# Where the large SBUF tiles of a gated decoder layer begin, counted in bytes

## Chip, core and metric

The kernel runs on one core of a Trainium2 chip. The metric is the device time of one execution in microseconds (us). Before the change three runs took 1215.79, 1216.19 and 1220.27 us; the median is 1216.19 us.

## The reference, cut to what matters

One decoder layer over 1024 positions, model width 1024, everything in float32:

```python
h = rmsnorm(x, mix_norm)
q, k, v, su, sv, g_a, g_b = split(h @ w_in)
y_att = sliding_window_attention(q, k, v, q_norm, k_norm, sinks)   # window 128, ALiBi, sinks
y_sgu = chunked_spatial_gating(su, sv, sgu_norm, w_s, b_s)         # chunks of 128
merged = sigmoid(g_a) * (y_att @ w_oa) + sigmoid(g_b) * (y_sgu @ w_ob)
x = x + merged @ w_out
z = causal_conv3(rmsnorm(x, ffn_norm) @ w_up)                      # 1024 x 5632
gate, val = split(z)
x = x + (silu(gate) * val) @ w_down
```

## The kernel before

**Precision.** TensorE is fed with `float32r`. To keep float32 accuracy each operand is split into a high part and a low part, and each product is three matmuls: high by high, high by low, low by high (`mm3`, lines 79 to 81). Every matmul loads its own 128x128 stationary operand (the trace calls that LDWEIGHTS, on the row PEld), also when the next one uses the same again. The moving operand is 512 columns wide in the large stages and 256 in the projections for k, v, q and the gating input.

**Stages, in the order of time.** First the projections for k and v while x arrives. Then attention over 128-query blocks, with the q and u projections as filler work of TensorE. Then the gating input v (`v_half`, line 531: 256-column matmuls with moving tiles `wv` and `wvB`, stationary x). From about 261 us on all large work is in 512-column matmuls: 8 gate pairs, 16 branch products `po` (24 matmuls each), 8 output products `px` (48 each), 22 pairs of the MLP, and the down projection. The gate pairs and the MLP pairs use seven block products instead of eight (`Blocks.prod`, line 914: A11, A12, S1, A22, S2, S3, S4, of 12 matmuls each); the down projection uses seven as well (line 1595, 924 matmuls).

**Pools.** SBUF is handed out by pools, from the left and from the right, and each tile begins where the pool puts it. The tiles that TensorE reads come from these pools:

- `big` with tag `Y`: seven tiles of 16 KB in each partition, for the activations x, T1 to T4 and B, for `wq`, `wv`, `wkv`, for mh, ml, and for all four operands of the down projection (`ah`, `al`, `bh`, `bl`).
- `wst`, the weight pool: tiles `wh` and `wl` (line 93) of 4 KB, two of each; in the trace `ph`, `qh`, `wjh` are high parts and `pl`, `ql`, `wjl` low parts.
- S2 and S4 of the pairs (`AX`, `gax`) and S3 (`s3h`, `s3l`) are stationary operands too, but don't come from the weight pool: `AX` is a `Y` tile, the others are from smaller pools.
- `zr`, on the right: `wvB`, and later T3 of the gate pairs.

In the built program these tiles begin, as a remainder by 256 bytes:

```
Y tiles, wh, wl, s3h, s3l, gax, T3 of the MLP, vsh, vsl     32
wvB and T3 of the gate pairs (pool zr)                     224
ch, cl, eh, el of attention                                 64
```

All slices that a matmul takes of them are whole multiples of 512 bytes away from the tile's begin, so the remainder holds for each matmul's operand. Remainders 32 and 224 are both 32 by 64 bytes.

**Order.** The order of TensorE's work, and most of the others', is the order of the code (`manual_schedule`). Waits come from the tiles that instructions share.

Of the kernel before, what the change touches and what calls it, by code (L numbers as in the profile page):

```python
# [10 lines left out]
F = mybir.dt.float32  # L11
R = mybir.dt.float32r
U8 = mybir.dt.uint8
# [21 lines left out]
def build(tc, a):  # L35
    nc = tc.nc
    ctx = ExitStack()
    with ctx, tc.manual_schedule(engines={mybir.EngineType.PE}):
        body(ctx, tc, nc, a)


def body(ctx, tc, nc, a):
    L, H = slice(0, 512), slice(512, 1024)
    base = ctx.enter_context(tc.tile_pool(name="base", bufs=1))
    big = ctx.enter_context(tc.tile_pool(name="big", bufs=1))
    wst = ctx.enter_context(tc.tile_pool(name="wst", bufs=2))
    uid = [0]
# [26 lines left out]
    def copy_hi(dst, src, scale=1.0):  # L74
        return nc.scalar.activation(dst, src, AF.Copy, scale=scale)  # L75
# [37 lines left out]
    def rsqrt_cols(dst, ss, n, width):  # L113

        nc.vector.tensor_scalar(dst, ss, 1.0 / width, EPS, op0=ALU.mult, op1=ALU.add)
        return nc.gpsimd.tensor_tensor(dst, dst, mh05[:, :n], op=ALU.pow)

    msk = base.tile([128, 4, 128], U8, name="msk")

    def rms_rows(pb, diag, hs=(0, 1)):  # L120

# [2 lines left out]
        for h, p in zip(hs, pb):  # L124
# [9 lines left out]
    att = tc.tile_pool(name="att", bufs=1)  # L134
    at = att.__enter__()
    vhl = at.tile([128, 8, 2, 128], R, name="vhl")
    kgq = at.tile([128, 1], F, name="kgq")
    eps_x = at.tile([128, 8], F, name="eps_x")
    nsink = at.tile([128, 8], F, name="nsink")
    kp_cm = tc.tile_pool(name="kp", bufs=1, side="right")  # L140
    kp = kp_cm.__enter__()
    kTh = kp.tile([128, 2, 1024], R, name="kTh")
    kTl = kp.tile([128, 1024], R, name="kTl")
    ali = kp.tile([128, 8, 128], F, name="ali")
    nc.gpsimd.affine_select(out=ali[:, 0:4, :], in_=ones.unsqueeze(1).to_broadcast([128, 4, 128]),
                            pattern=[[0, 4], [1, 128]], compare_op=ALU.is_gt, fill=0.0, base=0,
                            channel_multiplier=-1)
# [40 lines left out]
    def xsquare(k):  # L188
        for c in (L, H):
            xs = xr[k][:, 257 + c.start:257 + c.stop]  # L190
            if k == 0:
                nc.scalar.activation(sqsum[:, c], xs, AF.Square)
                continue
            sq = PH("sq")
            nc.scalar.activation(sq, xs, AF.Square)
            nc.vector.tensor_tensor(sqsum[:, c], sqsum[:, c], sq, op=ALU.add)
# [35 lines left out]
        if k == 6:  # L232
            rsplit(wq[0], rwq[1], 1)
    xsquare(7)
    u_next = [wst.tile([128, 8, 128], R, tag="wh", name="u0h"), wst.tile([128, 8, 128], R, tag="wl", name="u0l")]
    copy_hi(u_next[0], u_raw[0])
    nc.vector.tensor_tensor(u_next[1], u_raw[0], u_next[0].bitcast(F), op=ALU.subtract)

# [1033 lines left out]
    def ssq_cols(p):  # L1272
        for s in range(8):
            nc.tensor.matmul(p[:, 2 * s:2 * s + 2], pools["sq2"][:, s * 128:(s + 1) * 128], ones[:, 0:2],
                             start=True, stop=True)
        pool = pools["fp"]
        ss = pool.tile([128, 8], F, name="ss8b")
        nc.vector.tensor_copy(ss, p[:, 0:16].rearrange("p (s two) -> p s two", two=2)[:, :, 0])
        rsqrt_cols(ss, ss, 8, D)
        nc.vector.reciprocal(rstd, rstd)  # L1280
        nc.vector.tensor_tensor(ss, ss, rstd, op=ALU.mult)
        diag = pool.tile([128, 8, 128], F, tag="ac", name="diag2", bufs=2)
        nc.vector.tensor_tensor(diag, ident.unsqueeze(1).to_broadcast([128, 8, 128]),
                                ss.unsqueeze(2).to_broadcast([128, 8, 128]), op=ALU.mult)
        return diag
# [80 lines left out]
    def first_pair():  # L1366
# [34 lines left out]
        nc.vector.tensor_tensor(q.g0, q.g0, x1, op=ALU.add)  # L1401
        pb = q2.zv
        diag = ssq_cols(pb)
        nx.sums_r()
        q.prod(q.v1, "S2", "T2", more=True)
# [379 lines left out]
```

## Time and profile before

| | |
|---|---|
| median of three runs | 1216.19 us |
| span of the profiled execution | 1218.1 us |
| PE busy | 1195.9 us, 98% of the span |
| DVE busy | 893.3 us, 73% |
| ACT busy | 542.1 us, 45% |
| POOL busy | 568.0 us, 47% |
| mean granted TensorE clock | 0.992 |

The page gives no time of the profiled execution other than its span; it is 1.9 us above the median of the runs. Matmuls overlap in the engine's pipeline, so a matmul's listed duration (389 ns for 512 columns) is not what it costs in a stream. What it costs is the distance from one start to the next, which has to be read from start times or from a count of instructions in a stretch.

### The profile page before, as it was taken

The numbers are of one execution on the slowest core, as the hardware profiler recorded it, in microseconds if no ns is written. First come the engines' busy times: TensorE is split into PE (matmuls) and PEld (weight loads), VectorE is DVE, ScalarE is ACT, GpSimd is POOL, SyncE is SP. The second block draws the span as 40 slices with busy tenths as digits, with TensorE's granted clock in tenths as the row PEclk, the third lists the DMA queues.
The fourth block names the chain that finished last, engine by engine and source line by source line (L and its number), as shares of the span: only waits on it lengthen the run. The fifth ranks groups of instructions, "written<-read, shape, count | busy, mean of one in ns | idle before, by whom it ended". The sixth has DMA issues, their size and how long they took to land.

```text
span 1218.1 us, 15838 instructions
## 1 busy us (share of the span) xinstructions
PE 1195.9 (98%) x5866; PEld 1004.7 (82%) x5866; DVE 893.3 (73%) x1033; ACT 542.1 (45%) x830; POOL 568.0 (47%) x358
## 2 busy tenths in 40 slices
PE   9999999889999999999999999999999999999998
PEld 8888889868887888888788888888888888888886
DVE  7788866874455665577798788887888888775674
ACT  8555566733434322223444444444444445424331
POOL 2466584278766522334756657566575642000000
PEclk9999999989999999999899999999999999999999
DMA  7010133125767897442223334233332347975471
GB/s 274 26 52 19 53 121 139 42 85 169 256 237 274 289 348 286 156 156 103 96 87 121 121 113 145 88 122 117 117 141 90 124 166 274 386 253 190 143 233 66
DMA packets 78989, 191.27 MB, mean 157 GB/s; under 512 B 8896, under 2 KB 9152, under 8 KB 78912
## 3 DMA queue, kind: packets, MB, share of 16 engines
q1 hardware_dynamic: 78912, 190.26, 44.3%
q8 instruction: 46, 0.75, 0.2%
q14 instruction: 31, 0.25, 0.1%
HBM read 139.63 MB, written 50.59 MB: 156 GB/s over the span
## 4 chain that ended last, share of the span: by engine, by line
PE 87%; DVE 6%; DMA 3%; ACT 2%; issue 1%; POOL 1%; SPq 0%; ACTq 0%; DVEq 0%
PE pz L914 42%; PE pd L1595 10%; PE pdy L1595 7%; PE px L81 2%; PE px L79 2%; PE po L79 2%; PE po L81 2%; PE po L80 2%; PE px L80 2%; DMA ls<-wup 2%; PE pv L498 1%; PE pu L81 1%; PE pu L79 1%; PE pu L80 1%; DVE T L750 1%; PE pq L79 1%
## 5 line engine op out<-in xcount | busy, mean ns | idle before, releaser
L914 PE MATMUL pz<-T,qh 128*128 128x512 f32 x464 | 142.8, 389 | 0.0
L879 POOL TENSOR_TENSOR pl<-lp,ph 128x1024 fp32r<-128x1024 f32 x30 | 73.6, 2455 | 85.0 <-ACT ph L75 84.9
L914 PE MATMUL pz<-B,ph 128*128 128x512 f32 x352 | 109.5, 392 | 0.0
L914 PEld LDWEIGHTS pz<-T,qh 128*128 128x128 f32 x464 | 87.2, 188 | 18.1
L914 PE MATMUL pz<-T,ql 128*128 128x512 f32 x232 | 90.3, 389 | 0.0
L96 POOL TENSOR_TENSOR wjl<-wj,wjh 128x512 fp32r<-128x512 f32 (+1 forms) x24 | 41.1, 1713 | 95.2 <-ACT wjh L75 95.2
L879 POOL TENSOR_TENSOR ql<-lq,qh 128x1024 fp32r<-128x1024 f32 x30 | 77.5, 2582 | 14.8 <-ACT qh L75 14.8
L914 PEld LDWEIGHTS pz<-B,ph 128*128 128x128 f32 x352 | 65.3, 188 | 15.5 <-ACT x L1443 1.9
L929 DVE TENSOR_TENSOR pz<-pz,rstd_b 128x1024 f32<-128x1024 f32 x60 | 73.9, 1232 | 3.0 <-ACT rstd_b L125 0.9
L879 POOL TENSOR_TENSOR s3l<-s,s3h 128x512 fp32r<-128x512 f32 x30 | 41.2, 1374 | 71.2 <-ACT s3h L75 67.0
L914 PE MATMUL pz<-T,s3h 128*128 128x512 f32 x232 | 71.7, 390 | 0.0
L914 PE MATMUL pz<-B,pl 128*128 128x512 f32 x176 | 68.6, 390 | 0.0
L1595 PE MATMUL pd<-bh,ah 128*128 128x512 f32 x176 | 68.5, 389 | 0.0
L1595 PE MATMUL pd<-bl,ah 128*128 128x512 f32 x176 | 68.5, 389 | 0.0
L1595 PE MATMUL pd<-bh,al 128*128 128x512 f32 x176 | 68.5, 389 | 0.0
L914 PE MATMUL pz<-T,AX 128*128 128x512 f32 x264 | 65.8, 400 | 0.0
L914 PE MATMUL pz<-B,AX 128*128 128x512 f32 x264 | 63.4, 389 | 0.0
L75 ACT ACTIVATE qh<-lq 128x1024 fp32r<-128x1024 f32 x30 | 31.9, 1063 | 66.7 <-issue 46.6
L914 PEld LDWEIGHTS pz<-T,AX 128*128 128x128 f32 x264 | 51.2, 194 | 10.8
L914 PEld LDWEIGHTS pz<-B,AX 128*128 128x128 f32 x264 | 49.6, 188 | 10.3
L1301 DVE SCALAR_TENSOR_TENSOR tg<-pz,cp,tg 128x1023 f32<-128x1023 f32 (+1 forms) x44 | 56.2, 1278 | 0.8
L1301 DVE SCALAR_TENSOR_TENSOR tv<-pz,cp,tv 128x1023 f32<-128x1023 f32 (+1 forms) x44 | 56.2, 1278 | 0.8
(333 smaller groups left out, 3556.9 us busy)
## 6 DMA issues: line engine op xcount, KB each, us to landing
ls<-wup SPq DMA_DIRECT2D x22, 512.0 KB, 5.9
sum<-ls SPq DMA_DIRECT2D x22, 512.0 KB, 5.3
lp<-wup SPq DMA_DIRECT2D x22, 512.0 KB, 3.6
ra<-wdown SPq DMA_DIRECT2D x44, 256.0 KB, 4.7
b<-T SPq DMA_DIRECT2D x44, 256.0 KB, 3.7
B<-tv SPq DMA_DIRECT2D x33, 256.0 KB, 2.0
T<-tt SPq DMA_DIRECT2D x33, 256.0 KB, 2.1
b<-B SPq DMA_DIRECT2D x33, 256.0 KB, 3.4
```

The costliest lines, as they stand in the source:

```text
L75: return nc.scalar.activation(dst, src, AF.Copy, scale=scale)
L79: nc.tensor.matmul(out, wh, mh, start=first, stop=False, **kw)
L80: nc.tensor.matmul(out, wh, ml, start=False, stop=False, **kw)
L81: nc.tensor.matmul(out, wl, mh, start=False, stop=last, **kw)
L96: nc.gpsimd.tensor_tensor(l[:, :nk, :], r[:, :nk, :], h[:, :nk, :].bitcast(F), op=ALU.subtract)
L498: nc.tensor.matmul(o, vhl[:, kb, g, :], w, start=i == 0, stop=i == len(ops) - 1)
L750: nc.vector.tensor_tensor(xb[n][:, 1, kk, :], src, xb[n][:, 0, kk, :].bitcast(F), op=ALU.subtract)
L879: nc.gpsimd.tensor_tensor(l, r, h.bitcast(F), op=ALU.subtract)
L914: nc.tensor.matmul(o, p[:, k, :], y[:, q, k, :], start=not more and k == 0 and j == 0, stop=k == 3 and j == 2, skip_group_check=True)
L929: nc.vector.tensor_tensor(z, z, rstd_b, op=ALU.mult)
L1301: nc.vector.scalar_tensor_tensor(t[:, j:], p[:, 0:1024 - j], cw[:, ci, 2 - j:3 - j], t[:, j:], op0=ALU.mult, op1=ALU.add)
L1595: nc.tensor.matmul(o[d], p[:, k - k0, m], q[:, k - k0, :], start=new and k == 0 and j == 0, stop=k == HK - 1 and j == 2, skip_group_check= ...
```

## The change

Only the places of tiles change. The rows of every engine and the semaphores that each row waits for are the same in both built programs, in the same order; the one name that differs is `ss8b`, which becomes `ss_b`.

- Pads are put in: 160 bytes in `base`, 480 bytes at the right edge, 64 bytes in `wst` ahead of the first `wh`, 128 bytes ahead of the first `wl`.
- Small tiles (`kgq`, `eps_x`, `nsink`, and `ss8b` as `ss_b`) move from `att` and `fp` to `base`; the mask `msk` moves from `base` to `kp`.

```diff
+    edge = ctx.enter_context(tc.tile_pool(name="edge", bufs=1, side="right"))
+    edge.tile([128, 120], F, name="edge_pad")
...
-    msk = base.tile([128, 4, 128], U8, name="msk")
+    kgq = base.tile([128, 1], F, name="kgq")
+    eps_x = base.tile([128, 8], F, name="eps_x")
+    nsink = base.tile([128, 8], F, name="nsink")
+    ss_b = base.tile([128, 8], F, name="ss_b")
+    base.tile([128, 40], F, name="base_pad")
...
-    kgq = at.tile([128, 1], F, name="kgq")
-    eps_x = at.tile([128, 8], F, name="eps_x")
-    nsink = at.tile([128, 8], F, name="nsink")
...
+    msk = kp.tile([128, 4, 128], U8, name="msk")
...
-    u_next = [wst.tile([128, 8, 128], R, tag="wh", name="u0h"), wst.tile([128, 8, 128], R, tag="wl", name="u0l")]
+    wst.tile([128, 16], F, name="wst_pad", bufs=1)
+    u_next = [wst.tile([128, 8, 128], R, tag="wh", name="u0h")]
+    wst.tile([128, 32], F, name="wst_pad2", bufs=1)
+    u_next.append(wst.tile([128, 8, 128], R, tag="wl", name="u0l"))
...
-        ss = pool.tile([128, 8], F, name="ss8b")
+        ss = ss_b
```

In the changed program the large tiles begin, as a remainder by 256 bytes:

```
Y tiles (with AX of the MLP)                                64
wh                                                         128
wl                                                           0
s3h, s3l, gax, T3 of gate pairs and MLP, wvB, vsh, vsl       0
```

All of these are multiples of 64 bytes. Seen from a `Y` tile, a high part of the weights begins 64 bytes further on, a low part 192 (by 256); `AX` beside `Y`, S3 beside T3, and the operands of the down projection among themselves keep a difference of 0.

## Rows read from the trace of the kernel before

**Rows 1.** The page: PE's line, and the chain that ended last
```profile
PE 1195.9 (98%) x5866; PEld 1004.7 (82%) x5866; DVE 893.3 (73%) x1033; ACT 542.1 (45%) x830; POOL 568.0 (47%) x358
...
PE 87%; DVE 6%; DMA 3%; ACT 2%; issue 1%; POOL 1%; SPq 0%; ACTq 0%; DVEq 0%
```

**Rows 2.** Waits of PE: who was waited for, us, times, longest
```profile
PE pe L914 <- DVE x L1012: 5.6, 1, 5.6
PE pm L79 <- ACT pm L809: 3.9, 2, 2.1
PE pz L1274 <- DVE sq L1394: 1.8, 1, 1.8
```

**Rows 3.** Stretches of MLP and down projection: busy (instructions), PEclk, DMA share, GB/s
```profile
700.00:800.00 100.00, 100.00 (x442) 1.00 0.36 125
1040.00:1140.00 100.00, 100.00 (x442) 1.00 0.74 255
```

**Rows 4.** Timeline of PE, v stage, moving wv: start us, length us
```profile
187.07 0.28 PE L79 MATMUL pvs<-wv,x 128*128 128x256 f32 x1
...
188.51 0.28 PE L79 MATMUL pvs<-wv,x 128*128 128x256 f32 x1
```

**Rows 5.** Timeline of PE, v stage, moving wvB
```profile
198.25 0.28 PE L79 MATMUL pvs<-wvB,x 128*128 128x256 f32 x1
...
199.61 0.28 PE L79 MATMUL pvs<-wvB,x 128*128 128x256 f32 x1
```

**Rows 6.** Timeline of PE, gate pair, product S3 with T3
```profile
286.91 0.63 PE L914 MATMUL pz<-T,s3h 128*128 128x512 f32 x2
...
289.71 0.62 PE L914 MATMUL pz<-x,ph 128*128 128x512 f32 x2
```

**Rows 7.** Timeline of PE, MLP, clock at the lower level
```profile
593.39 5.28 PE L914 MATMUL pz<-T,AX 128*128 128x512 f32 x12
598.50 0.63 PE L914 MATMUL pz<-T,qh 128*128 128x512 f32 x2
```

**Rows 8.** Groups by shape: busy us, mean ns of one
```profile
L1595 PE MATMUL pd<-bh,ah 128*128 128x512 f32 x176 | 68.5, 389 | 0.0
L1595 PE MATMUL pdy<-bh,ah 128*128 128x512 f32 x132 | 51.5, 390 | 0.0
L79 PE MATMUL px<-mh,wjh 128*128 128x512 f32 x128 | 49.8, 389 | 0.0
L79 PE MATMUL pu<-x,wuh 128*128 128x512 f32 x48 | 19.5, 407 | 0.0
L79 PE MATMUL pq<-wq,x 128*128 128x256 f32 x128 | 36.8, 288 | 0.4 <-DVE qs L282 0.4
```

**Rows 9.** Timeline of PE where the gates begin; idle before it, and for whom
```profile
260.81 1.19 PE L914 MATMUL pe<-T,qh 128*128 128x512 f32 x2 [5.59 <-DVE x L1012]
```

**Rows 10.** Stretches of DVE: busy (instructions), PEclk, DMA share, GB/s
```profile
245.00:260.00 15.00, 14.87 (x9) 0.90 0.04 16
400.00:600.00 200.00, 136.37 (x124) 0.98 0.57 208
700.00:800.00 100.00, 84.22 (x81) 1.00 0.36 125
```

**Rows 11.** Groups of DVE with tiles at remainder 0 (cl) and 32 (x)
```profile
L476 DVE TENSOR_TENSOR cl<-pt,ch 128x512 fp32r<-128x512 f32 x16 | 11.1, 691 | 6.0 <-ACT ch L75 5.5
...
L925 DVE TENSOR_TENSOR pz<-x,pz 128x512 f32<-128x512 f32 x29 | 20.2, 695 | 1.0
```

## The prediction

> **What bounds the kernel now.** I read the page first: PE is busy in 98% of the span and is 87% of the chain that ended last [rows 1]. Then I read what PE waits for: after the first stage little is left, and the longest wait is 5.6 us [rows 2]. So from 261 us on the time is the number of matmuls times the distance from one start to the next. That distance is the third view: in two stretches without a wait 442 matmuls of 512 columns began in 100 us, at granted clock 1.00, 100 / 442 = 226.2 ns each [rows 3]; the last one counted is cut by the window, and I use 226.7, the value between 100/442 and 100/441. The instructions' listed 389 ns [rows 8] are no price, since they overlap.
>
> The fourth view is the timeline of short stretches, and there the distance changes with where the operands begin, while shape, type and clock stay:
>
> - 256 columns, moving and stationary operand both at remainder 32 by 256 bytes: 12 matmuls from 187.07 to 188.51 us, 120.0 ns each [rows 4].
> - 256 columns, moving operand (`wvB`) at 224, stationary at 32: 12 matmuls from 198.25 to 199.61 us, 113.3 ns [rows 5].
> - 512 columns, both at 32: 226.7 ns [rows 3].
> - 512 columns, moving operand (T3 of the gate pairs) at 224, stationary at 32: 12 matmuls from 286.91 to 289.71 us, 233.3 ns [rows 6].
>
> The first and third differ by 256 columns and 106.7 ns, so a column costs 0.417 ns, which is one column for each period of the upper level, 2.4 GHz. 512 columns are then 213.3 ns, and what is left over is 13.3 ns for operands at the same remainder [rows 3, 4], 6.7 for `wvB` [rows 5] and 20.0 for T3 [rows 6]: one, two or three steps of 6.7 ns, the time of 16 columns, which are 64 bytes. At the lower clock level the same MLP matmuls take (598.50 - 593.39) / 12 = 426 ns [rows 7], the 512 columns at 1.2 GHz with nothing left over. So I read the steps as time lost in fetching operands when they are wanted at the full rate, in pieces of 64 bytes, and as something that the place of the operands sets.
>
> **The change part by part.** No instruction is added, removed or moved and no wait changes, so the whole of it is the price of the same instructions with operands elsewhere.
>
> *The price of an aligned begin.* All operands now begin half-way in a 64-byte piece; afterwards they begin at its edge. No row shows a stream of 512 columns with such operands. The bounds: it can lose at most the whole leftover, 13.3 ns; and the nearest row on the other side is T3's, 6.7 ns more than now. I take one step, 6.7 ns: a stream of 2048 bytes that begins half-way touches 33 pieces instead of 32, and `wvB`, which also begins half-way, keeps just one step [rows 5].
>
> *The price of the offset.* The second step I put down to moving and stationary operand being wanted from the same place at once, since two steps stand where both have remainder 32 and one where `wvB` differs [rows 4, 5]. Weights from the weight pool lose that meeting if it goes by the difference of the remainders; but T3, with the same difference as `wvB`, has one step more and not one less [rows 6]. Between losing the step (6.7) and keeping it (0) I take the middle, 3.3.
>
> *The sum from 261 us on.* The matmuls of 512 columns are 30 pairs of 84 (2520, line 914), 924 in the down projection (three times 176 + 132, [rows 8]), 384 for `po` and 384 for `px` (three times 128): 4212 (some 36 of the first gate pair begin before 261 us, and stay in this count). At 226.7 ns they are 954.8 us, and from the end of the 5.6 us wait at 260.8 [rows 9] to 1218.1 us there are 957.3 us; so nearly nothing else is in the way there. Stationary operands from the weight pool have 4 products of 12 in each of 30 pairs (1440) and all of `po` and `px`: 2208. The other 2004 (S2, S3, S4 and the down projection) have difference 0 after the change as before.
>
> - 2208 x 10.0 ns = 22.1 us (one step and the middle)
> - 2004 x 6.7 ns = 13.4 us (one step)
>
> *Before 261 us.* u has 192 matmuls of 512 columns (48 of them in [rows 8]), 1.9 us at 10.0 ns. q has 384 of 256 columns (three times 128, [rows 8]) and v with `wv` 192: 576 x 6.7 = 3.8 us. The sgu product (96) has 0.6. That is 6.3 us. But at 255 us PE stands and waits for DVE [rows 9], which is busy for 14.87 of the 15 us up to 260 [rows 10]; DVE's work before this depends on PE's only in part, so part of the gain becomes a longer wait. I count half, 3 us; the bounds are 0 and 6.3.
>
> *Other engines.* DVE's instruction with a tile at remainder 0 takes 691 ns for 128x512, one of the same shape with a tile at 32 takes 695 [rows 11]. So I give DVE, ACT and POOL no change (a bound of 4 ns each on 1033 DVE instructions is 4 us, off the path). They don't become the bound either: DVE is busy 84 of 100 us in the MLP [rows 10], and with PE 4% faster this would be 88%. DMA lands elsewhere, but no wait of PE from the gates on names it [rows 2]. The pads need no wait, and the mask's place in `kp` is given back when its last reader is long done.
>
> Sum: 22.1 + 13.4 + 3 = 38.5 us. The span of 1218.1 us becomes 1179.6; the span stands 1.9 us above the median of the runs, so against 1216.2 the time is **1178 us**.
>
> *A rule that speaks against it.* That two operands meet is what the rows suggest: 120.0 against 113.3 ns with nothing but the moving tile's place changed [rows 4, 5]. The Trainium skill (SBUF — State Buffer, "Who interferes with whom") says that PE has two read ports, one for the moving operand and one for the weights, independent of each other, and that PE never waits on anyone. By that the offset would be worth nothing, and 2208 x 3.3 ns = 7.3 us would go from the sum; the trace doesn't agree with it wholly, since it shows a place that matters.
>
> As for how low a stream may get, the leftover of 13.3 ns is the rows' [rows 3, 4]. The Trainium skill (TensorE: Matmul & The Clock Gate, "Back-to-back issue gap") gives N / 2.4 + 2.5 ns, an estimate of 215.8 ns for 512 columns; by this the 4212 matmuls would gain 45.9 us rather than 35.5. No run here shows such a stream.
>
> **The rivals.**
>
> *T3's case becomes the common one (slower).* T3's 233.3 ns [rows 6] is the only 512-column stream in which the stationary operand begins 64 bytes further on than the moving one (by 256), and after the change this holds for all loads of a high part beside a `Y` tile: two of three, 1472 of the 2208. If the difference sets the price and the edge of the 64 bytes does nothing, they gain a step: 1472 x 6.7 = 9.8 us. If the 736 loads of low parts do the same, it is 14.7 us. The 924 and the S matmuls stay. The time is 1226 to 1231 us. For it: the same difference, the same width. Against it: with 256 columns the same difference has a step less [rows 5]. It decides the sign where alignment gives less than 9.8 us / 4212 = 2.3 ns on each matmul.
>
> *Alignment alone.* The offset does nothing and each matmul loses half a step or one: 4212 x 3.3 to 6.7 = 14 to 28 us, 1188 to 1202 us with 0 to 3 us from before 261 us taken in. For it: the 6.7 ns step is 64 bytes. Against it: `wvB` shows that begins half-way in a piece don't all cost the same.
>
> *The place isn't the cause.* The steps could come from the slot in which a load falls into the stream: the streams in [rows 4 to 6] also differ in width and in what ran before. Then the same order gives the same slots, and the time stays 1216 us. Against it: 120.0 and 113.3 ns belong to the same code, ten us apart [rows 4, 5].
>
> *A chain on DVE or POOL eats it.* PE has few waits now [rows 2]; a gain of 35 us over 957 brings DVE to 88% in the MLP and to 71% between 400 and 600 us [rows 10], so this could cost some us at stage borders and not the whole. I put it into the range.
>
> **How the numbers follow.** Forecast (alignment and at least part of the offset, 1155 to 1187 us): 0.53. Alignment alone: 0.18. No effect: 0.11. T3's case: 0.18. The likeliest one's own range is 1155 to 1187: at the low end the whole leftover goes, 4212 x 13.3 = 56 us and 5 us before 261 us. The range that is to hold 8 times in 10 starts a little above this end and reaches over alignment alone and no effect, not over T3's case: 1157 to 1219 us. What this kernel's measurement can tell from no change is 0.5%, 6 us. Faster takes the forecast and nearly all of alignment alone, 0.70; within 0.5% no effect and a rest of the two, 0.13; slower 0.17.
>
> **What would show it.** In a stretch of 100 us of the MLP, 442 matmuls should become 455 to 465, and the timeline there should show high and low parts of the weight pool's products at about 217 ns and the products S2 to S4 at 220 (226.7 now). In the down projection the count should be near 454. `px` and `po` should show the same as the weight pool's products of the pairs. DVE's and ACT's mean durations should stay. The wait of PE for DVE before 261 us should grow by some us. The prediction is wrong if the down projection keeps 442 in 100 us (then alignment gives nothing), if products with weights from the pool are at 230 or above while the others fall (T3's case), or if the matmuls are faster and PE's waits took it back.

## The result, and the profile after

The changed kernel takes 1229.12 us (median of four runs, 1226.73 to 1231.52) against 1217.56 us for the kernel before, a ratio of 1.0097 with a 95% interval of 1.0078 to 1.0115. It is slower by about 1%, where 1178 us was forecast. That time lies where the rival on T3's case put it, at 1226 to 1231 us.

The page after, PE's line and the chain, beside [rows 1]:

```profile
PE 1207.8 (98%) x5866; PEld 1005.4 (82%) x5866; DVE 894.0 (73%) x1033; ACT 544.3 (44%) x830; POOL 569.6 (46%) x358
...
PE 85%; DVE 7%; ACT 3%; DMA 2%; issue 1%; POOL 1%; SPq 0%; ACTq 0%; DVEq 0%
```

PE's busy time grows by 11.9 us and the span by 10.3, since PE stands 1.6 us less than before; the other engines' busy times stay within 2.2 us. What PE waits for, beside [rows 2], stays as well, so no new wait was made:

```profile
PE pe L921 <- DVE x L1019: 5.4, 1, 5.4
PE pm L81 <- ACT pm L816: 3.9, 2, 2.1
PE pz L1281 <- DVE sq L1401: 1.3, 1, 1.3
```

The two stretches without a wait, beside [rows 3], tell where the time went:

```profile
700.00:800.00 100.00, 100.00 (x436) 1.00 0.35 118
1040.00:1140.00 100.00, 100.00 (x442) 1.00 0.78 272
```

In the MLP 436 matmuls begin in 100 us instead of 442. In the down projection, where all operands moved from remainder 32 to 64 together, there are 442 as before. The timeline of two products with weights from the weight pool (start us, length us):

```profile
712.76 0.62 PE L921 MATMUL pz<-T,qh 128*128 128x512 f32 x2
...
718.32 2.90 PE L921 MATMUL pz<-T,AX 128*128 128x512 f32 x12
```

24 matmuls take 5.56 us, 231.7 ns each instead of 226.7. T3's product in a gate pair, beside [rows 6], now has both operands at the same remainder, and its 12 matmuls take 2.77 us, 230.8 ns each:

```profile
288.69 0.63 PE L921 MATMUL pz<-T,s3h 128*128 128x512 f32 x2
...
291.46 0.63 PE L921 MATMUL pz<-x,ph 128*128 128x512 f32 x2
```

That is less than the 233.3 of before and not the 226.7 of an undisturbed stream; it stands between products whose weights are offset.

One more stream has an offset that neither the list of places nor the prediction counts: after the change `gax` begins at remainder 0 and the activations beside it at 64, which is a difference of 192. The first line is where its 24 matmuls of a gate pair begin, the second where the next product does:

```profile
280.31 2.96 PE L921 MATMUL pz<-T,gax 128*128 128x512 f32 x12
...
285.92 0.62 PE L921 MATMUL pz<-x,ph 128*128 128x512 f32 x2
```

That is 5.61 us for 24, 233.7 ns each; before the change they took 226.7.

Summed from start to start over the whole trace, in us:

```
                                   before    after
2208 with weights from the pool     503.6    514.3   +10.7
 923 of the down projection         209.3    209.5    +0.1
1080 with S2, S3, S4                257.7    256.7    -0.9
 192 of u                            45.1     45.4    +0.3
```

The first line, 4.8 ns on each of 2208 matmuls, is as large as the whole difference. The third hides a second loss: the 192 matmuls with `gax` lose 1.1 us in it, but its distances also hold waits, which are 1.9 us shorter, and fewer of its matmuls ran at the lower clock level. DVE's two groups of [rows 11] kept their 695 and 691 ns:

```profile
L932 DVE TENSOR_TENSOR pz<-x,pz 128x512 f32<-128x512 f32 x29 | 20.2, 695 | 1.0
...
L483 DVE TENSOR_TENSOR cl<-pt,ch 128x512 fp32r<-128x512 f32 x16 | 11.1, 691 | 6.0 <-POOL wgl L772 5.3 <-ACT ch L77 0.2
```

### The profile page after: what moved, and what is told of

It is laid out like the page before. It is cut to its first block, busy times and chain, and to the rows that moved or that the text cites. A ratio compares the mean times of both kernels' runs of the same rounds, so it can differ in the third digit from the quotient of the medians.

```text
span 1228.4 us, 15838 instructions
## 1 busy us (share of the span) xinstructions
PE 1207.8 (98%) x5866; PEld 1005.4 (82%) x5866; DVE 894.0 (73%) x1033; ACT 544.3 (44%) x830; POOL 569.6 (46%) x358
## 4 chain that ended last, share of the span: by engine, by line
PE 85%; DVE 7%; ACT 3%; DMA 2%; issue 1%; POOL 1%; SPq 0%; ACTq 0%; DVEq 0%
PE pz L921 43%; PE pd L1602 10%; PE pdy L1602 7%; PE po L83 2%; PE po L81 2%; PE po L82 2%; PE px L83 2%; PE px L81 2%; PE px L82 2%; PE pv L505 1%; PE pu L83 1%; PE pu L81 1%; PE pu L82 1%; DVE T L757 1%; PE pq L81 1%
## 5 line engine op out<-in xcount | busy, mean ns | idle before, releaser
L921 PEld LDWEIGHTS pz<-B,AX 128*128 128x128 f32 x264 | 49.6, 188 | 10.3
```

Source lines behind the costliest of these rows:

```text
L921: nc.tensor.matmul(o, p[:, k, :], y[:, q, k, :], start=not more and k == 0 and j == 0, stop=k == 3 and j == 2, skip_group_check=True)
```

## The experiments

"Difference" below is that between the starts of stationary and moving operand, by 256 bytes.

**Alignment alone.** Both pads of the weight pool stand behind its tiles, so weights and activations share remainder 64:

```diff
-    wst.tile([128, 16], F, name="wst_pad", bufs=1)
     u_next = [wst.tile([128, 8, 128], R, tag="wh", name="u0h")]
-    wst.tile([128, 32], F, name="wst_pad2", bufs=1)
     u_next.append(wst.tile([128, 8, 128], R, tag="wl", name="u0l"))
+    wst.tile([128, 16], F, name="wst_pad", bufs=1)
+    wst.tile([128, 32], F, name="wst_pad2", bufs=1)
```

> The changed kernel with both pads of the weight pool behind the low parts, so that weights and activations have the same remainder (64) and all large tiles still begin at multiples of 64. Theory D: 1216 us, no change from the kernel before (a step of nothing on 4212 matmuls), gax alone at some 232 ns (+1 us). Theory A of the prediction (an aligned begin gives 3 to 7 ns a matmul): 1188 to 1202 us. Theory O (something else of the change, the moved small tiles or the mask, costs the 10 us): 1227 us.

1217.6 us against 1216.04, ratio 1.0008 (0.9996 to 1.0019): no change. The stretches of [rows 3], now with every operand of the MLP's weight-pool products at a multiple of 64 bytes:

```profile
700.00:800.00 100.00, 100.00 (x442) 1.00 0.34 116
1040.00:1140.00 100.00, 100.00 (x442) 1.00 0.69 240
```

So the alignment is worth nothing that can be measured (at most 0.2% by the interval), and the small tiles that moved cost nothing. `gax` keeps its difference of 192 here, between products that have none, and takes 5.49 us for 24, 228.8 ns, where 232 was expected and 233.7 measured in the changed kernel:

```profile
277.83 2.91 PE L921 MATMUL pz<-T,gax 128*128 128x512 f32 x12
...
283.32 0.62 PE L921 MATMUL pz<-x,ph 128*128 128x512 f32 x2
```

So a short stream's price depends on its neighbours too, and not on its own difference alone.

**Offset alone.** The kernel before with the two pads and nothing else; no large tile begins at a multiple of 64:

```diff
-    u_next = [wst.tile([128, 8, 128], R, tag="wh", name="u0h"), wst.tile([128, 8, 128], R, tag="wl", name="u0l")]
+    wst.tile([128, 16], F, name="wst_pad", bufs=1)
+    u_next = [wst.tile([128, 8, 128], R, tag="wh", name="u0h")]
+    wst.tile([128, 32], F, name="wst_pad2", bufs=1)
+    u_next.append(wst.tile([128, 8, 128], R, tag="wl", name="u0l"))
```

> The kernel before with the two pads of the weight pool alone: activations at 32, high parts at 96, low parts at 224 by 256, none at a multiple of 64. Theory D: 1226 to 1229 us, weight-pool products at about 232 ns as in the changed kernel. Theory A: slower than the changed kernel by a further 3 to 7 ns on 2208 matmuls, 1234 us and more. Theory O: 1216 us.

1228.56 us, ratio 1.0104 (1.0085 to 1.0123), the changed kernel's within the intervals:

```profile
700.00:800.00 100.00, 100.00 (x436) 1.00 0.37 121
1040.00:1140.00 100.00, 100.00 (x443) 1.00 0.78 270
```

The two pads are the whole of the loss, at remainders 32, 96 and 224 as at 64, 128 and 0. They also push the pools behind the weight pool 192 bytes on, as in the changed kernel, so `gax` and S3 are as far from their activations here as there.

**Both parts 64 bytes on.** The changed kernel with `wst_pad2` behind the low parts:

```diff
     wst.tile([128, 16], F, name="wst_pad", bufs=1)
     u_next = [wst.tile([128, 8, 128], R, tag="wh", name="u0h")]
-    wst.tile([128, 32], F, name="wst_pad2", bufs=1)
     u_next.append(wst.tile([128, 8, 128], R, tag="wl", name="u0l"))
+    wst.tile([128, 32], F, name="wst_pad2", bufs=1)
```

> The changed kernel with high and low parts both 64 bytes further on than the activations (difference 64 in all of the weight pool's products, as T3 had in the kernel before). Theory D: 233.3 ns on 2208 matmuls, 1216 + 14.7 = 1231 us. Rival (the alternation of 64 and 192 costs, a constant difference doesn't): 1216 us or less.

1231.77 us, ratio 1.0126 (1.011 to 1.0143). In its MLP 21 matmuls begin in 717.81 - 712.91 = 4.90 us, 233.3 ns, T3's price of [rows 6]:

```profile
712.91 0.63 PE L921 MATMUL pz<-T,qh 128*128 128x512 f32 x2
...
717.81 0.63 PE L921 MATMUL pz<-T,qh 128*128 128x512 f32 x2
```

**T3 at difference 0.** The kernel before with a pad of 192 bytes at the right edge:

```diff
+    edge = ctx.enter_context(tc.tile_pool(name="edge", bufs=1, side="right"))
+    edge.tile([128, 48], F, name="edge_pad")
```

> The kernel before with a pad of 192 bytes at the right edge, which brings wvB and T3 of the gate pairs to remainder 32 as well, so that every 512-column stream but none of the attention has difference 0. Theory D: T3's 96 matmuls fall from 233.3 to 226.7 ns, 0.64 us; wvB's 192 rise from 113 to 120, 1.3 us, hidden before the wait for DVE; 1215 to 1217 us, no difference that can be measured. Rival S (the place only by chance): T3 stays at 233.

1217.75 us, ratio 1.0003 (0.999 to 1.0015), which can't be told from no change. The trace shows that the place sets the price all the same: T3's 12 matmuls take 2.72 us, 226.7 ns instead of 233.3 [rows 6], and `wvB`'s 192 rise from 113.9 to 120.0 ns on average:

```profile
288.42 0.62 PE L916 MATMUL pz<-T,s3h 128*128 128x512 f32 x2
...
291.14 0.62 PE L916 MATMUL pz<-x,ph 128*128 128x512 f32 x2
```

**Streams alone.** A program with nothing but streams of 72 or 144 matmuls in the kernel's pattern. A stream's name gives its starts in bytes: `m64` has all operands 64 on, `h64l192` the high parts of the stationary operand 64 and the low parts 192 further on than the moving operand, `d64` both parts 64. In the code, given in short, `m` is the moving operand's start, `h` and `l` are the differences of the high and low part:

```python
mh = M[:, m // 4 + n * k:m // 4 + n * k + n]
wh = W[:, (m + h) // 4 + 128 * k:(m + h) // 4 + 128 * k + 128]
nc.tensor.matmul(o, wh, mh, ...); nc.tensor.matmul(o, wh, ml, ...); nc.tensor.matmul(o, wl, mh, ...)
```

> Only streams of matmuls on one tile of moving and one of stationary operands, in the kernel's pattern (high by high, high by low, low by high), 40 streams with other starts; nothing of the layer is computed, the output is zeros. Theory D (the difference by 256 bytes between the moving operand and the stationary operand that is loaded meanwhile sets the price, the absolute start nothing): 512 columns with difference 0 take 226.7 ns whatever the start (m32, m64, m128 like d0), 64/192 takes about 232 as in the changed kernel, a constant 64 takes 233.3 as T3 took in the kernel before; d256 and d512 are as d0. Theory S (what sets it is the slot in which a load falls into the stream, and the place only by chance): streams with the same difference don't agree with those numbers. Theory A (the edge of 64 bytes counts as well): m32 is slower than d0 and m64. With 256 columns D expects 120 for 0 and 113.3 for 64. Open, with no number: whether some difference goes under 226.7.

The first matmul of each three (durations min/median/max, first and last start, so 69 matmuls from the first to the last time):

```profile
L71 PE MATMUL d0x<-mv,wt x24: 389/389/389, 33.8 to 49.4; 128*128 128x512 f32 x24
L71 PE MATMUL d64x<-mv,wt x24: 393/396/398, 50.1 to 66.2; 128*128 128x512 f32 x24
L71 PE MATMUL d192x<-mv,wt x24: 392/392/392, 83.6 to 99.4; 128*128 128x512 f32 x24
L71 PE MATMUL d256x<-mv,wt x24: 389/389/389, 249.9 to 265.5; 128*128 128x512 f32 x24
L71 PE MATMUL m32x<-mv,wt x24: 389/389/397, 282.5 to 298.2; 128*128 128x512 f32 x24
L71 PE MATMUL m64x<-mv,wt x24: 389/389/397, 298.9 to 314.5; 128*128 128x512 f32 x24
L71 PE MATMUL h64l192x<-mv,wt x24: 392/393/398, 331.6 to 347.6; 128*128 128x512 f32 x24
```

The mean distance in each stream's last half, in ns, from the start times:

| stream, 512 columns | distance |
|---|---|
| difference 0, starts 0, 32, 64 and 128; differences 256 and 512 | 226.7 |
| difference 64 | 233.4 |
| difference 128 | 232.4 |
| difference 192 | 229.0 |
| high parts 64, low parts 192 (the change) | 231.7 |
| differences 16, 240 and 252 | 226.7 |
| all other differences and pairs | 229.0 to 234.3 |

None is under 226.7. So the start by itself costs nothing, a difference costs 2 to 8 ns except for a few of those close to 0 (by 256), and the kernel before already had the best, T3's products aside. With 256 columns it is the other way round: difference 0 takes 120.0 and the others 117.8 to 118.7; `wvB`'s 113.3 [rows 5] did not come back here.

**What the leftover is.** Longer streams of 96, with the stationary operand cut to 64 or 32 columns, two PSUM banks in turn, the same stationary slice each time, other widths, and small differences:

```python
wh = W[:, (m + h) // 4 + 128 * kw:(m + h) // 4 + 128 * kw + p]      # p = 128, 64 or 32
nc.tensor.matmul(two[i % 2 if alt else 0], w, x, ...)
```

> Streams of 96 matmuls alone, nothing of the layer is computed, the output is zeros. What is open: why a difference of 4 took 232.4 ns and 16 took 226.7, and what the 13.3 ns over the 512 columns are that no place took away. Theory D with a lock (near difference 0 the two fetches fall into step and stay so; which cycle a stream ends in can depend on what ran before): d0 comes back to 226.7 after every other stream, d4 differs with its forerunner, 8 to 12 and 244 to 248 are at 226.7, 24 and 232 are not. Theory L (the 13.3 ns come from the load of the stationary operand running beside the stream): with 64 or 32 stationary columns they shrink to 7 or less. Rival F (they are a fixed cost of each matmul, as the handing over from one to the next): they stay at 13.3 with fewer stationary columns, and at widths 480, 448, 384, 320 and 256 the price is columns times 0.417 plus 13.3. Rival B (one PSUM bank as the target): with two banks in turn they shrink.

First and last start over 95 distances:

```profile
L72 PE MATMUL d0ax<-mv,wt x96: 389/389/397, 39.4 to 60.9; 128*128 128x512 f32 x96
...
L72 PE MATMUL p64x<-mv,wt x96: 387/391/398, 459.9 to 481.7; 128*64 128x512 f32 x96
L72 PE MATMUL altx<-mv,wt x96: 389/389/389, 526.5 to 548.1; 128*128 128x512 f32 x96
L72 PE MATMUL fwx<-mv,wt x96: 389/389/389, 570.1 to 591.6; 128*128 128x512 f32 x96
L72 PE MATMUL w384x<-mv,wt x96: 334/334/346, 653.8 to 670.3; 128*128 128x384 f32 x96
L72 PE MATMUL w320x<-mv,wt x96: 302/309/309, 670.5 to 684.4; 128*128 128x320 f32 x96
L72 PE MATMUL w256x<-mv,wt x96: 281/283/283, 684.6 to 696.0; 128*128 128x256 f32 x96
```

512, 384, 320 and 256 columns take 226.7, 173.3, 146.7 and 120.0 ns: columns times 0.417 plus 13.3 each time. It is no constant of every width: 480 and 448 take 16.6 and 16.0 more than their columns, and 128 takes 58.3 more. Two banks and a repeated slice don't change it. Fewer stationary columns make it worse, 230.0 with 64 and 231.7 with 32, so it doesn't come from the load's length; and at 512 columns no place among those tried takes it away.

What a difference costs depends on the width as well. A difference of 64 costs 6.7 ns at 512 columns (233.3) and 1.4 at 384 (174.7 against 173.3), and nothing at 448 (202.1 against 202.7):

```profile
L72 PE MATMUL w448x<-mv,wt x96: 361/365/369, 634.4 to 653.6; 128*128 128x448 f32 x96
L72 PE MATMUL w448d64x<-mv,wt x96: 360/363/369, 723.6 to 742.8; 128*128 128x448 f32 x96
```

Difference 0 came back to 226.7 after every other stream, and difference 12 took 226.7 as well. The theory of a lock failed at other points: 4 took 232.4 behind difference 0 and behind 64 alike, 8 took 230.6, and 244 and 248 took 233.3 where 226.7 was expected.

**Which two operands must agree.** The moving operand's start alternates between 0 and q. In `own` the stationary operand has its own moving operand's start; in `meet` that of the moving operand before it, beside which it is loaded (in the second program's first stream the loads begin at 39.2 us and the matmuls at 39.4, so a load runs about one matmul ahead). The lines in short:

```python
mo = q * (i % 2)
so = mo if own else q * ((i + 1) % 2)
```

> Streams of 96 matmuls of 512 columns alone, nothing of the layer is computed, the output is zeros. The moving operand's start alternates between 0 and q by 256. In the streams own-q the stationary operand has the start of its own moving operand, so the load that runs beside a stream differs from it by q; in meet-q it has the start of the moving operand before, so that what runs side by side agrees and what belongs together differs. Theory D with the load meanwhile: meet-q takes 226.7 ns for each q, own-q 229 to 234. Rival (own pair: what counts is the matmul's own two operands): own-q takes 226.7, meet-q 229 to 234. Rival (both, or the change of start from one matmul to the next): neither takes 226.7. d268 and d260 repeat differences 12 and 4 with 256 more: by D's period of 256 they take 226.7 and 232.4.

```profile
L69 PE MATMUL own64x<-mv,wt x96: 388/394/399, 59.8 to 81.8; 128*128 128x512 f32 x96
L69 PE MATMUL meet64x<-mv,wt x96: 389/393/398, 82.0 to 104.0; 128*128 128x512 f32 x96
...
L69 PE MATMUL d268x<-mv,wt x96: 393/394/397, 304.0 to 326.2; 128*128 128x512 f32 x96
L69 PE MATMUL d260x<-mv,wt x96: 387/392/400, 326.4 to 348.5; 128*128 128x512 f32 x96
```

| q | `own`, ns | `meet`, ns |
|---|---|---|
| 32 | 231.7 | 231.7 |
| 64 | 231.8 | 231.6 |
| 128 | 228.4 | 230.0 |
| 192 | 231.7 | 233.3 |

None is at 226.7: my theory that only the load running beside a stream must agree falls, and so does the rival that only a matmul's own two operands must. What the streams show is narrower: 226.7 came safely only where all starts in a stream agree by 256. d260 repeats difference 4 (232.3 against 232.4). d268 took 233.3, and so did d12 in this run, where d12 had 226.7 before. In this run it stood behind a stream of difference 64 and before behind one of 0, but the order of the operands differs between the two programs too, so which of these does it is not shown.

## Why the prediction was wrong

- **What bounds the kernel** held: PE's matmuls set the end. 2208 of them give 10.7 us where the span grows by 10.3. The rest nearly cancels: more for `gax`, less for waits.
- **The price of an aligned begin** is the step that failed first. It was set at one step, 6.7 ns on 4212 matmuls; it is nothing. Alignment alone gave a ratio of 1.0008, and the down projection, which got only that, kept its 442 in 100 us.
- **The price of the offset** failed in sign. Forecast was a gain of 3.3 ns on 2208 matmuls; it is a loss of 4.8 ns, and offset alone makes it.
- **The reading behind both** was that the 13.3 ns over the columns are time lost by the place of the operands, one step for the begin and one for the meeting. With equal starts they stay at every start tried and at widths 256, 320, 384 and 512; at 512 columns another place only adds to them. With that I had priced 512-column streams from a 256-column row, `wvB` [rows 5], and set aside the one 512-column row with an offset, T3 [rows 6], which had the sign right. The nearest row was the one of the same width.
- **The 2004 matmuls with difference 0 "as before"** were miscounted, in the section on the change too. 96 of them, S3 beside T3 of the gate pairs, had a difference of 64 before, and 192, those with `gax`, have one of 192 afterwards. This didn't decide the sign: it is 1.1 us lost at `gax` and some 0.2 us gained at T3.
- **Before 261 us** nothing was gained; the wait for DVE is 5.4 us instead of 5.6. **Other engines** kept their busy times within 2.2 us, as forecast.
- **T3's case**, at 0.18, came true in its cause (the difference costs, the edge does nothing) and in its time, the time in part by luck. Its terms were 6.7 ns on 1472 or on 2208 matmuls; measured are 4.8 ns on 2208, since with 64 and 192 mixed the price is 231.7 ns, and only the constant 64 gives 233.3 (1231.77 us).
- The rule that PE's two read ports are independent (the Trainium skill, SBUF — State Buffer, "Who interferes with whom"), taken as a rule for the time, does not agree with these runs: the stationary operand 64 bytes further on takes 233.4 ns, and both operands 64 bytes further on take 226.7, as at 0. The 2.5 ns over the columns (the Trainium skill, TensorE: Matmul & The Clock Gate, "Back-to-back issue gap") are given there for an isolated matmul and not for a stream, so they were no bound for this one. These float32r streams don't come near it: the least over the columns is 13.3 ns at 512 columns, and 6.7 in any row read here, `wvB`'s.

What stays open: what the 13.3 ns are, why 512-column streams with equal starts are the fastest while at 256 columns they are not, where in the chip the two operands meet, and how neighbours set the price of a short stream. No version tried beats the kernel before.

## What to carry to other kernels

Where TensorE runs float32r without a gap, read the distance from start to start in a stretch without waits for each pair of operands. For 512-column streams keep the pools such that moving and stationary tiles begin at the same place by 256 bytes; pads that break this cost 2% of those streams here (4.8 of 226.7 ns). Other widths need a reading of their own: at 448 columns a difference of 64 cost nothing, and at 256 it saved 2 ns. A pad in one pool also moves the pools behind it, as it moved `gax` here. Price a stream from a row of the same width: a 256-column row had the opposite sign. A leftover that looks like a loss may be a fixed cost, and a stream alone, with the start or the width as its only variable, tells the two apart in one run.

## What was not expected of the hardware

The distances within a stream are not all equal but repeat: 231, 236, 231, 235 ns at difference 64 in the first program, 233, 233, 234 in the second, with nearly the same mean (233.4 and 233.3); with equal starts they stay at 226 and 227.

A short stream between others needn't have the price of a long one. S3 with T3, 12 matmuls with equal starts, took 230.8 ns between offset products, and 226.7 where its neighbours had equal starts too. `gax`, 24 matmuls at a difference of 192, took 233.7 ns between offset products and 228.8 between products with equal starts; alone, in 72, a difference of 192 took 229.0.
